# A two-layer mixer and mixture-of-experts block on one core: another order for the opening of the experts, another grouping of routed tiles, and conditioning products in halves

## The chip, the cores and the metric

The kernel runs on one NeuronCore of a Trainium2 chip. The metric is the time of one execution on the device in microseconds; the kernel before took a median of 3143.61 us in three runs (3134.78 to 3149.41).

## The reference, cut to what matters

All arithmetic is float32. Two layers work on 1024 image tokens and 256 context tokens of width 1024. Layer 0 mixes with a gated linear recurrence in both directions, layer 1 with differential attention. Every layer first makes its six conditioning vectors and ends in a mixture of 32 experts, of which every token takes two from one of four groups:

```python
shx1, scx1, gx1, shx2, scx2, gx2 = jnp.split(silu(cond) @ w_mod[layer] + b_mod[layer], 6)
ox, oc = rglru_mixer(...) if layer == 0 else diff_attn_mixer(...)
x = x + gx1 * ox
hx2 = modulate(rms_norm(x, norm2_g[layer]), shx2, scx2)
s = sigmoid(h @ router_w)                        # 32 scores, two experts of the best group
y = sum over the two experts of weight * ((silu(h @ w_gate[e]) * (h @ w_up[e])) @ w_down[e])
x = x + gx2 * y
```

The matrix `w_mod` has 1024 x 6144 elements a layer. An expert has gate and up matrices of 1024 x 512 and a down matrix of 512 x 1024: 6 MB, so 32 experts are 201 MB a layer. Layer 0 routes 1280 tokens, layer 1 the 1024 image tokens.

## The kernel before, in words

The schedule is written out by hand: each engine runs its instructions in the order of the program, and waits are set by the tiles that are written and read. SP issues the loads of weights, POOL issues indirect transfers and many stores.

**Conditioning.** `mod_steps` (L165 on) works through rounds `(layer, r)` of 2048 columns of `w_mod`. A round has eight steps, one for each block of 128 rows; a step loads two tiles of 128 x 1024 and calls `mod_mm` (L143), whose four products of 32 x 512 go to the four 32-column quarters of the PE array and to the four 32-partition quarters of one PSUM bank. Rounds (0, 1), (0, 2), (1, 0), (1, 1), (1, 2) are fillers of layer 0's recurrence stage: after each piece of a projection one step of them is run on PE.

**Output projection and routing.** `post_mixer` goes through the tiles of 128 tokens (ten in layer 0, eight in layer 1). For a tile it computes the projection in two halves of 512 columns, adds each half to the residual (`resid`, L806 and L807), normalises (`norm`, L814 to L820, with the stores of the residual and of `h2d`), transposes, and computes the router's logits (L837). Routing is done for groups of tiles, given as (first tile, count): (0, 4), (4, 3), (7, 3) in layer 0 and (0, 4), (4, 3), (7, 1) in layer 1. After the logits of a group's last tile `router` (L854 to L895) picks two experts for each token on VectorE; `slots`, one call later, ranks the tokens of each expert with products on PE (L903 to L906), writes `row` (L911), adds the counts to `macc` (L913), and issues for each tile and each of the two picks one scatter from POOL (L917) into the slot table `slotd` in DRAM. Behind the last group the counts become blocks of 64 rows (`nblk`, L1019 to L1021). The first expert's six weight chunks of 1 MB are loaded into `raws` during this stage.

**Experts.** `moe` keeps a ring of 20 chunk buffers (`NM`), of which the first six (`NR`) hold the first expert. Buffers 12 to 15 lie in a pool (`pm`) on the left of SBUF, buffers 6 to 11 and 16 to 19 in a pool (`pr`) on its right, ten of 8 KB. On the right there lay before it, from the same end, the projection's weights (`gup`, 64 KB) and its transposed tiles (`pst`, 16 KB), then the routing's own tiles (`pd`). A buffer can be written when what lay there has been read.

The opening (L1219 on) is this: SP and POOL read five experts' block counts from `nblk` (`know`); VectorE clears the halves for gathered rows (L1222); SP loads chunks 6 to 19; POOL loads table 0 (the first 64 slots of every expert) in two halves of 64 partitions (L1076), VectorE halves it into row numbers (L1080), POOL gathers the first rows of expert 0 and of expert 1 (L1102), loads tables 1 to 4, VectorE halves those; PE transposes expert 0's rows (`x_t`, L1109), VectorE copies them (L1110); and POOL gathers expert 0's second rows, if it has more than one block.

Then the loop over the experts: for each block of 64 rows gate and up on PE (L1117, two 64-column halves of the array at once), SiLU on ScalarE, a product on VectorE, transposes, the down product (L1133), scaling on ScalarE (L1139) and an indirect store from POOL (L1141). The next rows' transposes and the previous block's down product are run between the gate and up products and their own transposes. When an expert is done SP refills its buffers.

Of the kernel before, what the change touches and what calls it, by code (L numbers as in the profile page):

```python
# [19 lines left out]
P = 128  # L20
D = 1024
KD = D // P
# [19 lines left out]
ORDER = [g * 8 + i for i in range(8) for g in range(4)]  # L42
NR = 6
NM = 20
B = P // 2
NB64 = 5

# [13 lines left out]
def model(ctx, tc, A, out):  # L61
    nc = tc.nc
# [13 lines left out]
    xd = dram.tile([T, D], F32, name="xd")  # L76
# [10 lines left out]
    side = const.tile([P, 1], F32, name="side")  # L87
    nc.vector.memset(side[:B], 0.0)
    nc.vector.memset(side[B:], 1.0)
    ones = const.tile([P, P], F32, name="ones")  # L90
# [17 lines left out]
    cs = modp.tile([P, KD, 32], F32, name="cs")  # L108
# [18 lines left out]
    def mod_load(l, r, j, eng):  # L127
        res = []
        for h in range(2):
            wm = modp.tile([P, 1024], F32, name="wm", bufs=5)  # L130
            c0 = r * 2048 + h * 1024
            eng.dma_start(wm, A["w_mod"][l].rearrange("(j p) n -> p j n", p=P)[:, j, c0:c0 + 1024])
            res.append(wm)
        return res
# [4 lines left out]
    def mod_bias(l, r, eng):  # L139
        for v in range(2):  # L140
            eng.dma_start(bmod[v:P:32, :], A["b_mod"][l, r * 2048:(r + 1) * 2048].rearrange("(g n) -> g n", g=4))

    def mod_mm(ps, wm, j):  # L143
        for g in range(4):
            nc.tensor.matmul(ps[32 * g:32 * g + 32, :], cs[:, j, :], wm[g // 2][:, (g % 2) * 512:(g % 2 + 1) * 512],
                             start=(j == 0), stop=(j == KD - 1), tile_position=(0, 32 * g))

    def mod_out(l, r, ps):
        mt = modp.tile([P, 512], F32, name="mt", tag="wm", bufs=5)
# [16 lines left out]
    def mod_steps(rounds, pspool, tag, eng, beng, rest, ctag):  # L166

        todo = []
        for l, r in rounds:
            nxt = mod_load(l, r, 0, eng)  # L170
            for step in todo:
                step()
                yield
            mod_bias(l, r, beng)
            for _ in range(rest):
                yield
            ps = pspool.tile([P, 512], F32, name="mps", tag=tag, bufs=1)
            for j in range(KD):
                cur = nxt
                if j + 1 < KD:  # L180
                    nxt = mod_load(l, r, j + 1, eng)
                mod_mm(ps, cur, j)
                if j + 1 < KD:
                    yield
            todo = [lambda l=l, r=r, ps=ps: mod_out(l, r, ps)]
            if r == 0:
                mt = mod_out(l, r, ps)

                def cols(l=l, mt=mt):
                    ps = pspool.tile([P, 512], F32, name="cps", tag=ctag[0], bufs=ctag[1])  # L190
                    mod_cols(l, mt, ps)

                todo = [cols]
            yield
        for step in todo:
            step()
# [63 lines left out]
    raws = {}  # L260
# [425 lines left out]
    def post_mixer(l, N, variant, prep, w_src, x_src, x_dst, groups, w_col=None, head=None, early=None):  # L686
# [332 lines left out]
        nc.tensor.matmul(ct[:, :E], ones, macc, start=True, stop=True)  # L1019
        nc.vector.tensor_scalar(nblk, ct[:, :E], float(B - 1), None, op0=OP.add)  # L1020
        nc.vector.tensor_scalar(nblk, nblk, 6, None, op0=OP.arith_shift_right)  # L1021
# [15 lines left out]
    def x_in(t):  # L1037
        return A["x"][0, t * P:(t + 1) * P, :] if t < XT else A["ctx"][0, (t - XT) * P:(t - XT + 1) * P, :]

    mraw = post_mixer(0, T, lambda t: 0 if t < XT else 1, st0, A["rg_w_out"][0], x_in,  # L1040
                      lambda t: xd[t * P:(t + 1) * P, :], [(0, 4), (4, 3), (7, 3)],
                      early={"w": early, "st": sty, "finish": finish, "release": release})

    def moe(l, N, mraw, raws, keep=False):
# [5 lines left out]
        ps = pool("psM", space=PSUM)  # L1050
        ends = [(6 * E + c) % NM for c in range(4)]
        raws = raws + [(pm if i in ends else pr).tile([P, 2 * D], F32, name=f"wr{i}") for i in range(NR, NM)]
        tabs = pm.tile([P, NB64, E, 3], I32, name="tabs")
        flat = pm.tile([P, 1, 3], I32, name="tabj")
        halves = [w[:, i * 512:(i + 1) * 512] for w in wide for i in range(2)]
# [3 lines left out]
        hm = pm.tile([P, F], F32, name="hm")  # L1059
        ht = pm.tile([P, KF, B], F32, name="ht")  # L1060
        yms = [pm.tile([P, F], F32, name=f"ym{i}") for i in range(2)]
        curs = [pm.tile([P, 3], I32, name=f"cur{i}") for i in range(3)]
        p_x = ps.tile([P, 4, P], F32, name="p_x")
        p_g = ps.tile([P, F], F32, name="p_g")
        p_h = ps.tile([P, KF, B], F32, name="p_h")
        p_y = ps.tile([P, F], F32, name="p_y")
# [3 lines left out]
        h2v = h2d[l][0:N, :].rearrange("n (h d) -> (n h) d", h=2)  # L1070
        ydv = yd[l][0:2 * N, :].rearrange("n (h d) -> (n h) d", h=2)

        def tab_load(j0, j1):

            for h in range(2):
                nc.gpsimd.dma_start(tabs[h * B:(h + 1) * B, j0:j1],  # L1076
                                    slotd[l][j0 * B * E:j1 * B * E, :].rearrange("(j p e) c -> p j e c", p=B, e=E))

        def halve(t):
            nc.vector.tensor_scalar(t[:, :, 0:2], t[:, :, 0:2], 2.0, side, op0=OP.mult, op1=OP.add)  # L1080

        def load(k):

            raw = raws[k % NM]
            e, c = k // 6, k % 6
            if e < E:
                if k < NM:
                    w_chunk(l, raw, ORDER[e], FIRST[c])
                else:
                    with tc.If(used[e] > 0):  # L1090
                        w_chunk(l, raw, ORDER[e], FIRST[c])
            elif keep and k - 6 * E < N // (2 * P):
                c = k - 6 * E
                t = raw.rearrange("p (a d) -> p a d", a=2)
                nc.sync.dma_start(t, xd[2 * c * P:2 * (c + 1) * P, :].rearrange("(a p) d -> p a d", p=P))
                last[2 * c], last[2 * c + 1] = t[:, 0, :], t[:, 1, :]

        def chunk(e, c, j):
            return raws[(6 * e + FIRST.index(c)) % NM].rearrange("p (j f) -> p j f", j=j)

# [5 lines left out]
        def x_t(xb):  # L1106
            xv = xb.rearrange("t (p j) -> t j p", j=4)
            for j in range(4):
                nc.tensor.transpose(p_x[:, j, :], xv[:, j, :], ident)  # L1109
            nc.vector.tensor_copy(xt, p_x)  # L1110
# [50 lines left out]
        def rows_of(e, b):  # L1161
            return xfs[e % 2] if b == 0 else x1s[e % 2] if b == 1 else xms[b % 2]

        def fetch(e, b):

            if e < E:
                if b == 0:
                    gather(rows_of(e, b), tab(e, b)[:, 0:1])
                else:
                    with tc.If(rows[e] > b):  # L1170
                        gather(rows_of(e, b), tab(e, b)[:, 0:1])
# [15 lines left out]
        def finish(e, b, prev):  # L1187
# [27 lines left out]
            with more.Else():  # L1215
                turn(nxt, *prev)
                nc.gpsimd.tensor_copy(curs[e % 2], tab(e, b))

        for e in range(5):  # L1219
            know(e)  # L1220
        for xb in halves:
            nc.vector.memset(xb, 0.0)  # L1222
        for k in range(NR, NM):
            load(k)
        tab_load(0, 1)
        halve(tabs[:, 0])
        fetch(0, 0)
        fetch(1, 0)
        tab_load(1, NB64)
        for j in range(1, NB64):  # L1230
            halve(tabs[:, j])
        x_t(rows_of(0, 0))
        fetch(0, 1)
        for e in range(E):
            n = count(ORDER[e])
            know(e + 5)
# [373 lines left out]
    class last_head:  # L1610
        ps = psF
# [125 lines left out]
```

## Time and profile before

| | us |
|---|---|
| median of three runs | 3143.61 |
| lowest, highest | 3134.78, 3149.41 |
| profiled execution | 3148.4 |
| its span, first to last instruction | 3146.8 |
| PE busy | 2767.8 (88%) |
| VectorE busy | 1373.7 (44%) |
| ScalarE busy | 963.1 (31%) |
| POOL busy | 536.7 (17%) |
| gate and up products L1117, 3456 records | 771.7 |
| down products L1133, 1728 records | 411.7 |
| opening, layer 0: last projection's residual to first gate | 573.7 to 631.3 |
| opening, layer 1: first gate | 2395.6 |

The page's second part divides the span into 40 slices of 78.7 us. PE's digits are 5999989999499999999858999999998985999999991. They read as tenths of the slice in which PE worked. The row DMA gives the mean busy share of the core's 16 DMA engines in the same way. In rows in order of time the first number is the start in us from the span's beginning, the second how long it took; "x4" merges four instructions, and the bracket gives how long the engine stood idle before, and what ended that. A float32 product on PE leaves two records, so that "x8" is four products.

### The profile page before, as it was taken

The numbers are of one execution on the slowest core, as the hardware profiler recorded it, in microseconds if no ns is written. First come the engines' busy times: TensorE is split into PE (matmuls) and PEld (weight loads), VectorE is DVE, ScalarE is ACT, GpSimd is POOL, SyncE is SP. The second block draws the span as 40 slices with busy tenths as digits, with TensorE's granted clock in tenths as the row PEclk, the third lists the DMA queues.
The fourth block names the chain that finished last, engine by engine and source line by source line (L and its number), as shares of the span: only waits on it lengthen the run. The fifth ranks groups of instructions, "written<-read, shape, count | busy, mean of one in ns | idle before, by whom it ended". The sixth has DMA issues, their size and how long they took to land. (4 is left out here: it accounts for less than half of the span.)

```text
span 3146.8 us, 40433 instructions
## 1 busy us (share of the span) xinstructions
PE 2767.8 (88%) x14350; PEld 1703.6 (54%) x14350; DVE 1373.7 (44%) x2597; ACT 963.1 (31%) x1811; POOL 536.7 (17%) x762
## 2 busy tenths in 40 slices
PE   5999989499999999858999999998985999999991
PEld 3667668333333333347888888886872333333330
DVE  6566677411111111187666666666772111111115
ACT  4566652100010010145454544545430110001101
POOL 2121101211111111141101111010012111111113
PEclk8999999699999999969999999998997999999996
DMA  5556465478887897261000000003246877988544
GB/s 195 162 185 205 155 223 181 179 301 316 318 326 288 351 409 302 69 243 50 26 7 26 26 26 27 7 6 129 85 160 258 353 282 310 370 343 346 196 154 178
DMA packets 174213, 611.44 MB, mean 194 GB/s; under 512 B 27336, under 2 KB 80448, under 8 KB 126112
## 3 DMA queue, kind: packets, MB, share of 16 engines
q1 hardware_dynamic: 133328, 493.65, 41.0%
q0 software_dynamic: 40192, 111.96, 9.8%
q8 instruction: 218, 3.57, 0.5%
q14 instruction: 267, 2.19, 0.2%
q10 hardware_dynamic: 208, 0.07, 0.0%
HBM read 560.23 MB, written 64.22 MB: 198 GB/s over the span
## 5 line engine op out<-in xcount | busy, mean ns | idle before, releaser
L1117 PE MATMUL p_g<-wr,xt 128*64 128x512 f32 x3456 | 771.7, 598 | 47.6 <-ACT ym L1139 33.8
L1117 PEld LDWEIGHTS p_g<-wr,xt 128*64 128x64 f32 x3456 | 267.5, 137 | 469.2 <-issue 409.6
L1120 DVE TENSOR_TENSOR hm<-act,p_g 64x512 f32<-64x512 f32 x108 | 74.6, 691 | 832.8 <-ACT act L1119 832.8
L1133 PE MATMUL p_y<-wr,ht 128*64 128x512 f32 x1728 | 411.7, 612 | 23.5 <-issue 22.3
L1119 ACT ACTIVATE act<-p_g 64x512 f32<-64x512 f32 x108 | 63.5, 588 | 851.3 <-PE p_g L1117 851.3
L1133 PEld LDWEIGHTS p_y<-wr,ht 128*64 128x64 f32 x1728 | 118.7, 139 | 234.2 <-issue 220.2
L55 PE MATMUL qkv<-qwh,hth 128*128 128x384 f32 (+1 forms) x640 | 217.2, 339 | 1.3 <-ACT hth L1433 0.5
L56 PE MATMUL qkv<-qwh,htl 128*128 128x384 f32 (+1 forms) x640 | 211.1, 330 | 2.4 <-DVE htl L1438 1.4
L57 PE MATMUL qkv<-qwl,hth 128*128 128x384 f32 (+1 forms) x640 | 210.5, 329 | 0.6 <-DVE qwl L1288 0.6
L1528 DVE TENSOR_REDUCE st<-sc 128x1 f32<-128x1280 f32 x128 | 190.2, 1486 | 21.6 <-PE sc L1515 19.9
L1126 DVE COPY ht<-p_h 128x256 f32<-128x256 f32 x108 | 45.9, 425 | 344.1 <-PE p_h L1125 344.0
L1531 ACT ACTIVATE wide<-sc,st 128x1280 f32<-128x1280 f32 x128 | 168.8, 1324 | 66.2 <-DVE st L1528 66.2
L1554 PE MATMUL po<-V,wide 128*128 128x128 f32 x1280 | 166.6, 288 | 1.4 <-ACT wide L1548 0.5
L1102 POOL DMA_INDIRECT wide<-h2d,tabs x108 | 112.2, 1039 | 319.9 <-issue 70.8
L1554 PEld LDWEIGHTS po<-V,wide 128*128 128x128 f32 x1280 | 156.3, 201 | 13.1 <-ACT wide L1548 12.5
L1548 ACT COPY wide<-wtp 128x512 f32<-128x512 f32 (+1 forms) x192 | 87.8, 522 | 201.2 <-PE wtp L1547 201.1
L1109 PEld LDWEIGHTS p_x<-ident,wide 128*128 128x128 f32 x432 | 60.7, 210 | 141.0 <-issue 92.7
L1560 POOL DMA_DIRECT2D od<-ot x56 | 30.3, 540 | 623.4 <-ACT ot L1557 623.4
L1139 ACT ACTIVATE ym<-p_y,cur 128x512 f32<-128x512 f32 x64 | 44.0, 687 | 289.1 <-PE p_y L1133 226.3
L1512 PE MATMUL sc<-KT,QS 128*128 128x512 f32 (+1 forms) x384 | 117.1, 393 | 15.3 <-ACT KT L1362 11.8
L1109 PE MATMUL p_x<-ident,wide 128*128 128x128 f32 x432 | 81.1, 311 | 54.0 <-DMA wide<-h2d,tabs 48.2
L55 PEld LDWEIGHTS qkv<-qwh,hth 128*128 128x128 f32 x640 | 123.9, 194 | 3.0 <-issue 1.5
(353 smaller groups left out, 4611.2 us busy)
## 6 DMA issues: line engine op xcount, KB each, us to landing
wr<-in_moe_w_gate_dram SPq DMA_DIRECT2D x124, 1024.0 KB, 11.0
wr<-in_moe_w_up_dram SPq DMA_DIRECT2D x124, 1024.0 KB
wr<-in_moe_w_down_dram SPq DMA_DIRECT2D x124, 1024.0 KB, 17.6
wm<-in_w_mod_dram POOLq DMA_DIRECT2D x80, 512.0 KB, 5.5
cy<-yd SPq DMA_DIRECT2D x26, 512.0 KB, 6.9
qraw<-in_da_w_qkv_dram SPq DMA_DIRECT2D x48, 256.0 KB, 3.3
xd<-xres POOLq DMA_DIRECT2D x18, 512.0 KB, 3.9
h2d<-h POOLq DMA_DIRECT2D x18, 512.0 KB, 4.1
```

What stands on the lines that cost most here:

```text
L55: nc.tensor.matmul(ps, lh, rh, start=start, stop=False)
L56: nc.tensor.matmul(ps, ll, rh, start=False, stop=False)
L57: nc.tensor.matmul(ps, lh, rl, start=False, stop=stop)
L1102: nc.gpsimd.indirect_dma_start(out=dst, out_offset=None, in_=h2v, in_offset=bass.IndirectOffsetOnAxis(ap=idx, axis=0), bounds_check=2 * N ...
L1109: nc.tensor.transpose(p_x[:, j, :], xv[:, j, :], ident)
L1117: nc.tensor.matmul(p_g[i * B:(i + 1) * B, :], xt[:, j, h * B:(h + 1) * B], w[i][:, j, :], start=(h == 0 and j == 0), stop=(h == 1 and j == ...
L1133: nc.tensor.matmul(p_y[h * B:(h + 1) * B, :], ht[:, 2 * c + j, :], w[:, j, h * 512:h * 512 + 512], start=(c == 0 and j == 0), stop=(c == 1 ...
L1512: nc.tensor.matmul(o, qs[:, half, :], KT[b][:, half, c0:c0 + n], start=True, stop=False)
L1528: nc.vector.tensor_reduce(st[:, half:half + 1], sc_[:, half, :], AX.X, OP.max)
L1531: nc.scalar.activation(p, sc_[:, half, :], AF.Exp, bias=st[:, 2 + half:3 + half], scale=0.125, accum_out=st[:, 4 + half:5 + half])
L1548: nc.scalar.copy(wT[:, g * 4:g * 4 + n, :], pt[:, 0:n, :])
L1554: nc.tensor.matmul(po[:, 0:P], wT[:, k, :], V[h % 2][:, k, :], start=(k == 0), stop=(k == TT - 1))
```

## The change

Three things are changed.

- `mod_mm` takes a width. For layer 1 it is 256: a step's four products of 512 columns become eight of 256, first the left halves of all four quarters, then the right halves. Layer 0 keeps 512.
- Layer 0's tiles are routed in groups (0, 4), (4, 4), (8, 2).
- The opening of the experts has another order, in both layers. SP issues chunks 6 to 11 first. Table 0 is loaded by POOL and ScalarE, tables 1 to 4 by SP and ScalarE. Table 0 is halved, POOL gathers expert 0's first rows, tables 1 to 4 are halved, then the counts are read, and POOL gathers expert 0's second rows. ScalarE copies one element of those rows into the buffer of chunk 12. SP loads chunks 12 to 19, the first of which is written after that copy. Then come the transposes of expert 0's first rows and the gather for expert 1.

```diff
+NE = 12
...
-    def mod_mm(ps, wm, j):
-        for g in range(4):
-            nc.tensor.matmul(ps[32 * g:32 * g + 32, :], cs[:, j, :], wm[g // 2][:, (g % 2) * 512:(g % 2 + 1) * 512],
-                             start=(j == 0), stop=(j == KD - 1), tile_position=(0, 32 * g))
+    def mod_mm(ps, wm, j, width):
+        for c in range(0, 512, width):
+            for g in range(4):
+                nc.tensor.matmul(ps[32 * g:32 * g + 32, c:c + width], cs[:, j, :],
+                                 wm[g // 2][:, (g % 2) * 512 + c:(g % 2) * 512 + c + width],
+                                 start=(j == 0 and c == 0), stop=(j == KD - 1 and c + width == 512), tile_position=(0, 32 * g))
...
-                mod_mm(ps, cur, j)
+                mod_mm(ps, cur, j, 256 if l == 1 else 512)
...
-                      lambda t: xd[t * P:(t + 1) * P, :], [(0, 4), (4, 3), (7, 3)],
+                      lambda t: xd[t * P:(t + 1) * P, :], [(0, 4), (4, 4), (8, 2)],
...
-        def tab_load(j0, j1):
+        def tab_load(j0, j1, queues):
-            for h in range(2):
-                nc.gpsimd.dma_start(tabs[h * B:(h + 1) * B, j0:j1],
+            for h, eng in enumerate(queues):
+                eng.dma_start(tabs[h * B:(h + 1) * B, j0:j1],
                                     slotd[l][j0 * B * E:j1 * B * E, :].rearrange("(j p e) c -> p j e c", p=B, e=E))
...
+        for k in range(NR, NE):
+            load(k)
+        for xb in halves:
+            nc.vector.memset(xb, 0.0)
+        tab_load(0, 1, (nc.gpsimd, nc.scalar))
+        tab_load(1, NB64, (nc.sync, nc.scalar))
+        halve(tabs[:, 0])
+        fetch(0, 0)
+        for j in range(1, NB64):
+            halve(tabs[:, j])
         for e in range(5):
             know(e)
-        for xb in halves:
-            nc.vector.memset(xb, 0.0)
-        for k in range(NR, NM):
+        fetch(0, 1)
+        nc.scalar.copy(raws[NE][0:1, 0:1], rows_of(0, 1)[0:1, 0:1])
+        for k in range(NE, NM):
             load(k)
-        tab_load(0, 1)
-        halve(tabs[:, 0])
-        fetch(0, 0)
+        x_t(rows_of(0, 0))
         fetch(1, 0)
-        tab_load(1, NB64)
-        for j in range(1, NB64):
-            halve(tabs[:, j])
-        x_t(rows_of(0, 0))
-        fetch(0, 1)
```

## Rows read from the trace of the kernel before

**Rows 1.** busy time by stretch; columns: us, each engine's busy us (instructions), PEclk, DMA share, GB/s.

```profile
605.00:610.00 5.00, 0.00 (x0) 0.00 (x0) 0.00 (x0) 0.00 (x0) 0.38 (x1) 0.50 1.01 422
...
2370.00:2396.00 26.00, 1.54 (x6) 1.03 (x8) 4.00 (x11) 1.05 (x1) 6.30 (x8) 0.50 0.96 365
```

**Rows 2.** instructions in order of time, opening of layer 0's experts; start us, us, engine, line.

```profile
596.87 1.01 POOL L917 DMA_INDIRECT slotd<-row  x1 [13.74 <-DVE macc L913]
...
599.56 0.33 SPq L681 DMA_DIRECT2D wr<-in_moe_w_gate_dram  x1
...
603.31 0.96 POOL L917 DMA_INDIRECT slotd<-row  x1 [0.22 <-issue]
...
609.62 1.14 POOL L1076 DMA_DIRECT2D tabs<-slotd  x2 [5.34 <-DMA slotd<-row]
...
616.34 0.25 DVE L1080 TENSOR_SCALAR tabs<-tabs,side 128x64 int32<-128x64 int32 x1 [14.70 <-DMA tabs<-slotd]
617.39 1.11 POOL L1102 DMA_INDIRECT wide<-h2d,tabs  x1 [6.63 <-DVE tabs L1080]
...
624.50 1.13 PE L1109 MATMUL p_x<-ident,wide 128*128 128x128 f32 x4 [26.62 <-DMA wide<-h2d,tabs]
629.94 0.74 DVE L1080 TENSOR_SCALAR tabs<-tabs,side 128x64 int32<-128x64 int32 x4 [13.35 <-DMA tabs<-slotd]
...
631.33 1.12 PE L1117 MATMUL p_g<-wr,xt 128*64 128x512 f32 x2 [5.70 <-DVE xt L1110]
```

**Rows 3.** order of time, layer 1: routing of one tile, last scatter, first expert.

```profile
2361.27 0.19 DVE L859 TENSOR_TENSOR sm<-sc,rbt 128x32 f32<-128x32 f32 x1
...
2367.93 0.16 DVE L911 SCALAR_TENSOR_TENSOR row<-rank,ei 128x2 int32<-128x2 f32 x1
...
2369.64 0.98 POOL L917 DMA_INDIRECT slotd<-row  x1 [0.22 <-DVE nblk L1021]
...
2388.71 1.14 PE L1109 MATMUL p_x<-ident,wide 128*128 128x128 f32 x4 [19.77 <-DMA wide<-h2d,tabs]
...
2395.59 9.02 PE L1117 MATMUL p_g<-wr,xt 128*64 128x512 f32 x32 [5.74 <-DVE xt L1110]
```

**Rows 4.** PE's waits in layer 0's expert loop: us in total, times, longest.

```profile
PE p_y L1133 <- issue: 14.2, 4, 4.1
```

**Rows 5.** order of time, end of layer 0's output projection and its last routing.

```profile
554.55 0.25 DVE L859 TENSOR_TENSOR sm<-sc,rbt 128x96 f32<-128x96 f32 x1
...
557.70 1.04 PE L830 MATMUL pt<-ident,h 128*128 128x128 f32 x8
...
562.23 0.69 DVE L806 TENSOR_TENSOR o<-o,gate 128x512 f32<-128x512 f32 x1
...
569.42 0.69 DVE L806 TENSOR_TENSOR o<-o,gate 128x512 f32<-128x512 f32 x1
...
573.74 0.69 DVE L806 TENSOR_TENSOR o<-o,gate 128x512 f32<-128x512 f32 x1
...
587.21 0.26 DVE L859 TENSOR_TENSOR sm<-sc,rbt 128x96 f32<-128x96 f32 x1 [6.15 <-ACT sc L854]
...
596.42 0.17 DVE L911 SCALAR_TENSOR_TENSOR row<-rank,ei 128x6 int32<-128x6 f32 x1
```

**Rows 6.** DMA issues of the whole span; KB each, then median us from issue to landing.

```profile
od<-ot POOLq DMA_DIRECT2D x56, 64.0 KB, 1.9
...
slotd<-row POOLq DMA_INDIRECT x36, 2.1
```

**Rows 7.** line L1102 from 2900 to 2930 us, two row gathers: issue to landing.

```profile
DMA to landing us min/median/max: 2.8/5.3/7.8
```

**Rows 8.** order of time, layer 0: the fourth gate and up run.

```profile
667.44 7.09 PE L1117 MATMUL p_g<-wr,xt 128*64 128x512 f32 x32 [0.56 <-ACT ym L1139]
```

**Rows 9.** order of time, PE: one conditioning step of layer 1 and what follows.

```profile
252.25 1.07 PE L145 MATMUL mps<-wm,cs 128*32 128x512 f32 x8
253.25 0.50 PE L55 MATMUL ps_u<-hth,wh 128*128 128x512 f32 x1
```
## The prediction, before the result was known

> **What bounds the kernel now.** I read the profile from coarse to fine. The page's slices first: PE is nearly full but at both ends and in two slices inside the span, both where a layer's experts begin. Next the busy time by stretch: in the 26 us before layer 1's experts PE works 1.54 us while the DMA engines are 0.96 busy, and in layer 0's opening they stand at 1.01 with 422 GB/s [rows 1]. So in these two places the kernel waits for transfers. The order of time then shows for which: in layer 0 PE's first instruction of the experts waits 26.62 us for the gathered rows, and 5.70 us more for VectorE [rows 2]; layer 1 has 19.77 and 5.74 [rows 3]. Behind the opening PE is the bound: its largest wait in layer 0's loop after those two and the short hand-overs from ScalarE is 14.2 us in four pieces that no instruction or transfer ends [rows 4], and none is for weights. A microsecond won in the opening therefore stays won if weights still come in time.
>
> The opening of layer 0 in its order [rows 2]: six last scatters of slots begin at 596.87, the sixth at 603.31. Chunk loads begin at 599.56, behind the counts, and fill the DMA engines. The first table loads are issued at 609.62, land at about 616.3, the gather goes at 617.39 and lands at 624.5. The transposes run at once, but the copy of their result stands on VectorE behind the halving of tables 1 to 4, which waits for its own loads until 629.94. Gate and up begin at 631.33.
>
> **The change, part by part.**
>
> *Groups (4, 4) and (8, 2) in layer 0.* Before, the router of the three-tile group holds VectorE from 554.55 to 562.23 and delays tile 8's second residual, whose product PE has finished by 557.70 [rows 5]. That router goes, so tile 8's residual and norm, which ended when tile 9's first residual began at 569.42 [rows 5], end 4.3 us earlier, near 565.2. Then comes that residual (two instructions of 0.69, 1.4), and now the four-tile router. A tile costs a router and its slots (9.21 - 6.66) / 2 = 1.28 us: three tiles take 587.21 to 596.42 [rows 5], one takes 2361.27 to 2367.93 [rows 3]. Four tiles are thus 7.7 + 1.3 = 9.0, ending at 575.6, where tile 9's second residual stood at 573.74: 1.9 us late, and its norm, transposes and logits with it. The last router has two tiles, 1.3 less. The first last scatter comes at 596.87 + 1.9 - 1.3 = 597.5; the second group's eight scatters follow tile 9's stores on POOL, at 1.29 each, and end near 595, so they are out of the way. Four scatters instead of six: the last starts at 597.5 + 3 x 1.29 = 601.3, 2.0 us earlier than before.
>
> *Six chunks early.* Their buffers lie where the projection's weights and tiles lay (six of 8 KB in the 64 + 16 KB of those pools), all read for the last time before 573.74 (the last product's residual). They need no count, so SP issues them some 25 us earlier; 6.3 MB at 422 GB/s are 15 us, over near 590, behind a routing that uses no transfer in its chain. In layer 1 the same lies ahead of its router. Cost nothing; without this cover (buffers free only at the end of the routing) it is the second case below.
>
> *Quiet tables and gathers.* From the last scatter's start to the first gate, with empty engines:
> 1. the scatter lands: 2.1, median of 36 [rows 6];
> 2. the queue reacts: 0.7 (POOL took 0.8 from the end of the halving to the gather [rows 2]);
> 3. tables land, now from POOL, ScalarE and SP side by side: at least 1.9, like the small stores of attention [rows 6]; at most the 6.7 of before (609.62 to 616.34 [rows 2]); I take 2.4, near the quiet end, since nothing else is in flight;
> 4. halving and gather issue: 1.05 [rows 2];
> 5. the gather lands: 2.8 is the least seen, in a quiet moment [rows 7], 7.1 that of before [rows 2]; I take 3.2;
> 6. transposes, copy, first gate: 1.1 + 0.3 + 0.7 = 2.1, the halving of tables 1 to 4 being over, as their loads went beside the first.
>
> Together 11.6 us. Layer 0: 601.3 + 11.6 = 612.9 against 631.33, so 18.4 less. Layer 1, whose groups are unchanged: 2369.64 + 11.6 = 2381.2 against 2395.59, 14.4 less [rows 3].
>
> *What is late next.* The wait added is on ScalarE: a copy of one element reads the second gather's rows and writes chunk 12's buffer, so SP's last eight loads stand behind that gather. Behind the copy on ScalarE is only the first SiLU, 9 us after the gate begins. On POOL the gather of second rows now follows five register reads (about 2 us): issued near 611, landed near 614, needed at 612.9 + 9. SP then loads 8.4 MB at 422 GB/s, 20 us, until about 635. The third expert, whose run is the fourth (expert 0 has two blocks), began 36.1 us behind the first [rows 2, 8]; its first four chunks are wanted at 649.0. That leaves over 15 us. Expert 0's buffers come free 18 us earlier too, and their reloads queue some 5 us behind, with 30 us to spare.
>
> *Conditioning of layer 1 in halves.* 24 steps (3 rounds of 8), each with eight products of 256 columns instead of four of 512. A step takes PE from 252.25 to 253.25, 1.0 us [rows 9], in which four quarter tiles stream together. Two records of 512 columns in two rounds are 2 x 0.44 (32 records on two half tiles run in 7.09 us [rows 8], so 16 rounds of 0.44); 0.12 is left for entry and drain. The streamed columns stay the same, so the least change is -0.12 a step and the most twice that more, if each extra round pays all of it: -3 to +6 us. I take +0.05 a step, 1.2 us, all of it on the path, since PE is full there. The Trainium skill, "TensorEngine Tiling (Array Packing)", Instruction Overhead, speaks against short pieces: about 60 cycles for each matmul. An estimate from that page is 8 more records x 25 ns x 24 = 4.8 us; the sum would then be 3.6 us worse. No row here has pieces of this width on quarter tiles.
>
> **Sum.** 18.4 + 14.4 - 1.2 = 31.6 us. The profiled execution took 3148.4 us (span 3146.8 and 1.6 around it); it would take 3116.8. It lies 4.8 above the median of the runs, 3143.6, so on that scale I predict 3112.
>
> **The rivals.**
> *The traffic stays.* If the early six buffers wait until the routing is over, tables and gather still meet loads and only VectorE's wait goes: per layer 4.7 us (gate 2.1 behind the transposes of 624.50 and 2388.71, against 631.33 and 2395.59: 4.7 and 4.8), plus 2.0 for the earlier scatters, less 1.2: 10.3, so 3133. For it: these buffers were never used early. Against: the sizes of the pools, and that loads went from 599.56 on while scatters still read the routing's tiles [rows 2].
> *Weights late.* If the eight held loads start only at 646, the third expert waits 7 us in both layers: 3126. It decides from 639 on (649 less 10 us for four chunks); I see the hold end at 615.
> *Slower: quarter tiles no longer overlap at 256 columns.* Then a step is 4 x 0.88 = 3.5 us, 2.5 more, 24 times 60 us: 3112 + 59 = 3171. It decides once a step costs 2.3 us where it costs 1.0 now (24 x 1.3 = 31). Against: the tiles are independent and issued back to back.
> *PE's unexplained stalls.* The 14.2 us of layer 0 in four pieces [rows 4] lie amid straight products. If their place follows the place of the code, the products added ahead of it can move them: with twice as many, and layer 1 like layer 0 at most, up to 28 us, 3140 at worst, or as much won. The Trainium skill, "Runtime: NRT & Kernel Launch", Instruction fetch mechanics, says that a taken branch to code outside the fetched pages stalls the engine; no row shows it here.
>
> **How the numbers follow.** Forecast 0.76; traffic stays 0.09; weights late 0.05; tiles apart 0.07; stalls 0.03. The likeliest alone spans 3100 to 3124. With both landings at their upper ends (4.3 + 3.9 in each layer) and the halves at +6 it is 3133, with all at their lower ends 3106, and stalls moving by two of 3.6 us each reach 3099. I set 3098 to 3131. What a measurement can tell from no change is 0.5%, 15.7 us, thus 3128: faster 0.76 + 0.05 = 0.81; same, 0.09 + 0.03 = 0.12; slower 0.07.
>
> **What would show it.** Right: six loads of SP issued near 574 and near 2343; eight more only after a ScalarE copy, near 615 and 2384; tables landing within 3 us; the four halvings ahead of the transposes; first gate some 11.6 us after the last scatter's start; conditioning steps at 1.05 us. Wrong: a first gate over 16 us after the last scatter, a PE wait before the third expert, steps above 1.3 us.

## The result, and the profile after

The changed kernel's median is 3124.55 us (3113.12 to 3128.07) beside 3148.18 for the kernel before on the same chip: a ratio of 0.9926, interval 0.991 to 0.9941. Measured once more it had 3120.29 beside 3148.86, 0.9912 (0.9894 to 0.993). The forecast was 3112 beside 3143.6, a ratio of 0.9899. So the change is faster, by some 24 to 29 us (0.7 to 0.9%) where 31.6 was expected, and 3124.55 lies inside the range.

The profiled execution took 3128.07 us (span 3126.5), 20.3 less than before. Where they came from, in us, each stretch from the same instruction in both traces:

```
stretch                                     before    after    change   forecast
start to routing's first rank product       529.3     530.1     +0.8    +1.2 (halves)
rank product to layer 0's first gate        102.0      83.5    -18.5   -18.4
layer 0's experts                           694.2     686.4     -7.8     0
to layer 1's last scatter                  1044.1    1046.6     +2.5     0
last scatter to layer 1's first gate         26.0      11.4    -14.5   -14.4
layer 1's experts                           689.0     706.0    +17.0     0
tail                                         62.2      62.4     +0.2     0
```

Both openings came out as worked; what the forecast lacks lies in layer 1's expert loop, which it had left at its length. Layer 0's loop, left at its length too, came out 7.8 us shorter.

The two openings by stretch (us, each engine's busy us, PEclk, DMA share, GB/s), the answer to [rows 1]:

```profile
603.00:612.00 9.00, 0.26 (x1) 0.26 (x2) 1.00 (x5) 0.00 (x0) 2.70 (x3) 0.50 0.23 58
2348.00:2357.00 9.00, 0.81 (x4) 0.73 (x4) 2.49 (x9) 0.00 (x0) 3.13 (x4) 0.50 0.21 58
```

The DMA engines are 0.23 busy where they were full. Layer 0's opening in order of time, the answer to [rows 2] (start us, us, engine, line; in brackets the idle time before and what ended it):

```profile
572.26 0.33 SPq L684 DMA_DIRECT2D wr<-in_moe_w_gate_dram  x1
...
597.95 0.97 POOL L920 DMA_INDIRECT slotd<-row  x1 [3.49 <-DVE macc L916]
...
601.76 0.97 POOL L920 DMA_INDIRECT slotd<-row  x1 [0.23 <-issue]
603.96 1.26 ACTq L1079 DMA_DIRECT2D tabs<-slotd  x2
604.02 0.70 SPq L1079 DMA_DIRECT2D tabs<-slotd  x1
604.48 0.59 POOL L1079 DMA_DIRECT2D tabs<-slotd  x1 [1.75 <-DMA slotd<-row]
607.03 1.06 DVE L1083 TENSOR_SCALAR tabs<-tabs,side 128x64 int32<-128x64 int32 x5 [4.60 <-DMA tabs<-slotd]
608.18 1.10 POOL L1105 DMA_INDIRECT wide<-h2d,tabs  x1 [3.12 <-DVE tabs L1083]
...
611.75 1.13 PE L1112 MATMUL p_x<-ident,wide 128*128 128x128 f32 x4 [13.00 <-DMA wide<-h2d,tabs]
...
613.66 1.12 PE L1120 MATMUL p_g<-wr,xt 128*64 128x512 f32 x2 [0.78 <-DVE xt L1113]
```

From the last scatter's start to the first gate 11.9 us, 28.0 before. The tables go 2.2 after the scatter and land in 3.0, the gather lands 3.6 after its issue, all five halvings are over before the transposes, and the gate waits 0.78 for the copy. Layer 1 has the same picture in 11.4, the answer to [rows 3], with the element copy behind the second gather and the held loads behind that:

```profile
2346.68 0.97 POOL L920 DMA_INDIRECT slotd<-row  x1 [0.21 <-issue]
...
2356.19 1.13 PE L1112 MATMUL p_x<-ident,wide 128*128 128x128 f32 x4 [10.21 <-DMA wide<-h2d,tabs]
...
2358.03 0.19 ACT L1235 COPY wr<-wide 1x1 f32<-1x1 f32 x1 [23.15 <-DMA wide<-h2d,tabs]
2358.10 4.54 PE L1120 MATMUL p_g<-wr,xt 128*64 128x512 f32 x10 [0.78 <-DVE xt L1113]
...
2358.25 0.34 SPq L684 DMA_DIRECT2D wr<-in_moe_w_gate_dram  x1
```

A conditioning step of layer 1 in the order of time, pieces of 256 columns, the answer to [rows 9]:

```profile
410.13 1.07 PE L147 MATMUL mps<-wm,cs 128*32 128x256 f32 x16
411.13 0.50 PE L56 MATMUL ps_y<-hth,wh 128*128 128x512 f32 x1
```

1.00 us to the next product, as before: sixteen records stream in the time of eight. PE's waits in the two loops (us in total, times, longest), first layer 0's, the answer to [rows 4], then layer 1's, and last layer 1's in the kernel before:

```profile
PE p_y L1136 <- issue: 7.4, 3, 2.6
PE p_x L1112 <- issue: 3.6, 6, 1.0
...
PE p_y L1136 <- issue: 10.7, 4, 2.8
PE p_x L1112 <- issue: 7.6, 6, 5.1
...
PE p_y L1133 <- issue: 8.1, 3, 3.2
```

No line there waits for the landing of weights. The pieces that no instruction or transfer ends are still there, but at other places, and with one of 5.1 us in layer 1. The experiments are about these.

### The profile page after: what moved, and what is told of

It is laid out like the page before. It is cut to its first block, busy times and chain, and to the rows that moved or that the text cites. A ratio compares the mean times of both kernels' runs of the same rounds, so it can differ in the third digit from the quotient of the medians.

```text
span 3126.5 us, 40919 instructions
## 1 busy us (share of the span) xinstructions
PE 2770.1 (89%) x14542; PEld 1709.2 (55%) x14542; DVE 1374.5 (44%) x2597; ACT 964.4 (31%) x1813; POOL 532.8 (17%) x756
## 5 line engine op out<-in xcount | busy, mean ns | idle before, releaser
L1144 POOL DMA_INDIRECT yd<-ym,tabs x44 | 44.0, 1000 | 491.0 <-POOLq L1193 309.4
L56 PE MATMUL o<-wh,sth 128*128 128x512 f32 x288 | 118.9, 413 | 7.4 <-DVE xres L810 5.1
```

Source lines behind the costliest of these rows:

```text
L56: nc.tensor.matmul(ps, lh, rh, start=start, stop=False)
```

## The experiments

In all of them theory A is that these waits follow the place of PE's code. Counted from 0 in the traces, the runs of gate and up in a layer (54) give each wait an address that does not depend on the time: 26y is the wait among the down products behind the gates of run 26, x is one at the transposes of the rows, h one at those ahead of the down product, g one at the gates. PE's compiled program is 24576 bytes longer in the changed kernel than with 512 columns; the trace shows instruction packets of 16384 bytes on their own queue, so "place" below is the shift against 512 columns alone, less whole packets. Waits over 1.5 us, without those that a transfer or VectorE ends, from one profiled execution of each kernel:

```
kernel        place   layer 0                        layer 1                               loops, us
before          192*  7y 26y 30y 48y                 5y 19h 25y 52y                        694.2 689.0
w512              0   7y 26y 30y                     26g 52y                               685.0 689.7
pad64             0   7y 26y 30y                     5y 26g 52y                            681.6 687.5
w512_nohold       0   7y 26y 30y 34x                 5y 26g 52y                            686.4 692.5
w512_g33        -64   7y 24x 29y 39y                 20g 26g 39g 52y                       690.3 690.3
w512_pad32     4096   1x 5x 10y 34y 44y              21y 30y 44y 46g                       699.2 687.9
changed        8192   2y 35y 42y                     1x 12y 14g 22y 31y 45y                686.4 706.0
changed_again  8192   2y 20y 35y 42y                 1x 12y 22y 26g 31y 45y                687.1 702.4
w512_pad64     8192   2y 20y 35y 42y                 1x 12y 22y 26g 31y 45y                685.3 698.4
nohold         8192   14h 20y 35y 42y                12y 22y 26g 31y 45y                   685.2 693.7
late6          8192   2y 14h 20y 35y 42y             1x 12y 14g 22y 26g 31y 45y            690.3 697.7
only256        8384*  14y 20y 22y 36y 39x 42y        1g 13y 23y                            704.9 694.7
w512_pad96    12288   18g 22y 24y 28y 39x 40g        23y 36g                               688.9 686.7
* with the opening and the groups of before, whose program is 192 bytes longer than with the new ones
```

The traces bear out the places. Ahead of the loops, where PE's code runs straight, about one packet begins for every 128 of PE's records. Ahead of layer 0's first gate one begins 426 records before it in w512 and in pad64, and in w512_pad32, the changed kernel and w512_pad96 it begins 26, 61 and 91 records earlier than that, where the bytes, at 128 a record, give 32, 64 and 96.

They also show what ends the waits. The loops of the thirteen kernels hold 94 waits over 1.5 us that no instruction or transfer ends. In each of the 94 one packet of the instruction queue comes to its end, and PE goes on 1.17 to 1.73 us later. Such a packet takes about 1 us; the longer waits are those in which it begins late, up to 3.03 us after PE has stopped. Most packets cost nothing of the kind: layer 1's loop in the changed kernel sees 75 of them. The g waits are put down to PE's own sequencer, and a packet ends in each of these too, 2.07 to 2.26 us before PE goes on; not so 1g of only256, which is one of the 94, and 26g of layer 1. The last ends on a branch of SyncE's around a chunk's load (SPq L1093), stands there at both places, takes 1.2 us in the changed kernel too, and is no wait of this kind.

**w512: 512 columns again.**

```diff
-                mod_mm(ps, cur, j, 256 if l == 1 else 512)
+                mod_mm(ps, cur, j, 512)
```

> The changed kernel with layer 1's conditioning back in pieces of 512 columns; nothing else differs. Theory A (the forecast's missing 10 us are stalls of PE whose place follows the place of its code): the two openings keep 11.9 and 11.4 us from the last scatter to the first gate, a conditioning step is 1.00 us either way, and yet the experts' loops (686.4 and 706.0 us in the changed kernel) come out different by 4 to 15 us each, since 96 products fewer lie ahead of them; the whole anywhere between 3112 and 3140. Rival B (the pieces themselves cost time that the step does not show): both loops as in the changed kernel within 3 us, and the whole 8 to 12 us shorter, near 3114.

3107.95 us, ratio 0.9893 (0.9873 to 0.9912); loops 685.0 and 689.7, both openings as in the changed kernel (11.85 and 11.53). The steps stand at 1.00:

```profile
410.23 1.06 PE L147 MATMUL mps<-wm,cs 128*32 128x512 f32 x8
411.22 0.50 PE L56 MATMUL ps_y<-hth,wh 128*128 128x512 f32 x1
```

So the gain of leaving the pieces out is not in the step but in a loop 1900 us later. The ratio is the lowest of the study, though not told apart from that of w512_g33, and its interval touches those of the changed kernel. The time alone fits B better (some 6 to 10 us by the ratios); A's own bounds are missed, with layer 0's loop only 1.4 us from the changed kernel's, layer 1's 16.3, and the whole below 3112. The places speak for A, since all waits but 26g are at places of the kernel before, and B's equal loops are not there. Separating them needs the next runs.

**pad64: 64 more small transposes at the start of the changed kernel.**

```diff
+    for _ in range(64):
+        nc.tensor.transpose(vps[:, :16], crow, ident[:16, :16])
     nc.tensor.transpose(vps[:, :16], crow, ident[:16, :16])
```

> The changed kernel with 64 more of the first small transpose (16 by 16) at the start, where PE has no work for 11.5 us; they write the same values again. Theory A (place of the code): nothing moves before the first loop, the openings stay, but the stalls of PE in the two loops come at other points and the loops differ from 686.4 and 706.0 by 4 us or more, either way; largest single stall still 2 to 5 us. Rival C (the stalls come from what the loops do: the held loads, the order of experts): they come at the same experts, within 3 us the same loops, and the time is that of the changed kernel, 3125.

3112.93, ratio 0.9908 (0.9886 to 0.9931). The pieces of 256 are all there, and yet layer 1's loop is 687.5 and not 706.0. The 64 transposes add 8192 bytes, 24576 + 8192 are two packets exactly, and every long wait stands at a run where w512 or the kernel before has one: by the loops B and C fall, and A gets its sharp form. The whole time can't decide it: this ratio is not told apart from the changed kernel's 0.9912 in its second measurement, and the profiled execution, 3108.49, is among the fast ones of six (3106.81 to 3120.8). The transposes are not free, as I had expected: the 64 take 6.97 us, and the first product behind them comes at 19.44 and not 14.81, some 2 us late at the output projection.

**w512_pad64, w512_pad32, w512_pad96: the same pad with 512 columns.** The edit is the one above, with 64, 32 and 96, on w512.

> Layer 1's conditioning back at 512 columns, and 64 of the small transposes added at the start: PE's code then ends 8192 bytes later than with 512 columns alone, which is where the changed kernel has it, within one 16384-byte packet of the instruction queue (there 24576 bytes later, by 96 more products). Theory A, sharpened (a stall comes where a branch of PE's loop meets the seam of such a packet, so only the place modulo 16384 bytes counts): the stalls of the changed kernel come back, at 36, 187, 451 and 545 us behind layer 0's first gate and at 25 (5 us, beside the held loads), 168, 301, 421 and 599 us behind layer 1's; loops near 686 and 706; the whole near 3122, 12 to 15 us longer than with 512 columns alone. Rival B (the pieces of 256 columns cost the time by themselves): as with 512 columns alone, stalls at 98, 337 and 393 us behind layer 0's first gate, loops near 685 and 690, the whole near 3108.

3126.19, ratio 0.9937 (0.9916 to 0.9957): with the columns of before, the slow layer 1 of the changed kernel (698.4, beside 706.0 and 702.4 in its two profiles), and the list of its second profile run by run. This interval and w512's (0.9873 to 0.9912) do not meet. Its profile is 18 us longer than w512's (by the ratios it is some 14): about 2 are the pad itself and 9 the loops; the rest lies in the routing of layer 0 (3) and between the layers (4), and was not followed up.

> 512 columns and 32 of the small transposes at the start, 4096 bytes more of PE's code, a place that no kernel has had. Theory A, sharpened: stalls at other points than in either family (98, 337, 393 or 36, 187, 451, 545 us behind layer 0's first gate), a loop that is 0 to 10 us off 685 and 690; openings as before, 11.9 and 11.5 us. Rival B: the points and loops of 512 columns alone, 3108 within 3 us.

3128.33, 0.9939 (0.9917 to 0.9961). New places, as A says; layer 0's loop is 14 longer than w512's, more than the 10 that I allowed, with waits of 4.7 and 5.3 us at 1x and 5x.

> 512 columns and 96 of the small transposes, 12288 bytes more of PE's code. Theory A, sharpened: a fourth set of points, loops 0 to 10 us off 685 and 690, 3100 to 3125. Rival B: 3108 within 3 us, with the points of 512 columns alone.

3116.05, 0.9902 (0.9884 to 0.9919). A fourth list, and the loops within 4 us of w512's; the pad's own cost (10.4 us of transposes at the start, 5.5 of it still there at the output projection) makes most of the rest.

**only256: the kernel before with the pieces alone.** The edit is the diff's first part.

> The kernel before with nothing changed but layer 1's conditioning in pieces of 256 columns: PE's code gets 24576 bytes longer, one and a half packets of 16384. Theory A: a step costs 1.00 us as before, the openings stay at 28 and 26 us, and the stalls of PE's loops leave the points of the kernel before (100, 339, 396 and 623 us behind layer 0's first gate) for those of the changed one (187, 451 and 545; in layer 1 168, 301, 421 and 599). No stall of 5 us at 25 in layer 1, since no held loads are under way there. The whole 3135 to 3152. Rival B (the pieces cost time by themselves): 8 to 12 us longer than before, 3151 to 3156, with the points of the kernel before.

3164.4 beside 3148.86, ratio 1.0048 (1.0032 to 1.0065). Slower by more than either theory said. Chains of 28.2 and 25.3 us as before; loops longer by 10.7 and 5.7. The waits have left the list of before, which B cannot give; but only some of them are at those of the changed kernel (20y, 42y), so a list is fixed for one program, not for a place of the packet alone to 192 bytes. In w512_g33, 64 bytes from w512, only 7y of layer 0's three is kept, and 24x, 29y and 39y are new. How a list comes about inside a packet is open. PE's waits of layer 0's loop, against the 14.2 in 4 of before:

```profile
PE p_y L1135 <- issue: 17.0, 6, 4.8
```

**nohold and w512_nohold: without ScalarE's copy.**

```diff
-        nc.scalar.copy(raws[NE][0:1, 0:1], rows_of(0, 1)[0:1, 0:1])
```

> The changed kernel without ScalarE's one-element copy, so that SP's eight chunk loads follow the tables at once, near 606 us, and run beside the gathers. Theory D (the hold is what keeps the gathers quiet): the first gather takes 5 to 8 us instead of about 3, the first gate comes 2 to 5 us later in each layer, the whole 4 to 10 us longer, 3129 to 3135. Rival C (the held burst of eight loads is what stalls PE, as in the 5.1 us in front of layer 1's first transposes for the second run of an expert): the gates stay within 1 us, that stall goes and layer 1's loop is 5 us or more shorter, near 3118. Theory A has the stalls of the loops move by nothing, since no PE instruction is added or removed.

3121.16, 0.9926 (0.9904 to 0.9947). Both theories hold in part. The first gates come 15.8 and 15.5 us behind the scatters; the order of time in layer 0, where the loads had begun 1.6 us before the gather:

```profile
605.33 1.09 POOL L1105 DMA_INDIRECT wide<-h2d,tabs  x1 [3.19 <-DVE tabs L1083]
...
612.75 1.13 PE L1112 MATMUL p_x<-ident,wide 128*128 128x128 f32 x4 [16.90 <-DMA wide<-h2d,tabs]
```

The gather lands 7.4 us after its issue, beside 3.6 in quiet. So the hold is worth 3.9 and 4.1 us in the chains, as D says; but the whole is not longer, as C says: the ratio is that of the changed kernel, and layer 1's loop is 693.7 where that had 706.0 and 702.4. And of the five lists at place 8192 this one alone lacks the 1x of layer 1. The same transposes in the changed kernel, in its second run, in w512_pad64 and, last, in nohold:

```profile
2382.97 1.10 PE L1112 MATMUL p_x<-ident,wide 128*128 128x128 f32 x4 [5.11 <-issue]
```

```profile
2378.84 1.10 PE L1112 MATMUL p_x<-ident,wide 128*128 128x128 f32 x4 [5.08 <-issue]
```

```profile
2388.43 1.10 PE L1114 MATMUL p_x<-ident,wide 128*128 128x128 f32 x4 [5.21 <-issue]
```

```profile
2380.82 0.72 PE L1112 MATMUL p_x<-ident,wide 128*128 128x128 f32 x4 [0.31 <-issue]
```

Place and burst make this one together: w512 has the burst and not the place, and at its run there is no wait at all:

```profile
2373.12 0.75 PE L1112 MATMUL p_x<-ident,wide 128*128 128x128 f32 x4
```

In the changed kernel PE stops at 2377.86. Its traffic from 2376 to 2382 (forty slices, then the instruction packet):

```profile
DMA  9797999999799999997969596939592612023111
...
q8 instruction: 1, 0.02, 1.1%
```

That packet begins at 2380.42, when the held loads have just drained, and PE goes on at 2382.97; in nohold it begins at 2378.08, ahead of the need. That the fetch queued behind the burst is my reading of these times; the trace does not show when it was asked for. Nor does such a length need the held loads: w512_g33 has 5.5 us at 24x and w512_pad32 5.3 us at 5x, both in layer 0 and among the loop's own loads. The DMA engines are busy at a share of 0.96 or more around 93 of the 94 waits.

> 512 columns and no copy on ScalarE, so the eight later loads follow the tables at once. Theory D (the hold keeps the gathers quiet; its burst hurts only where a packet of PE's instructions is fetched in it, which with 512 columns it is not): first gates 15.8 and 15.5 us behind the last scatters, not 11.9 and 11.5, loops near 685 and 690 as with the hold, the whole 6 to 9 us longer than with it, 3114 to 3117. Rival C (the burst itself delays the loops): what the gates lose comes back in the loops, 3108 within 3 us.

3118.6, 0.9904 (0.9884 to 0.9925); gates 16.2 and 15.5 behind the scatters, the loops 4 longer together. As D says, with a little more: at a place without 1x the hold gains some 8 us in the chains. By the ratios the whole is 3.5 us longer than w512, within the noise.

**late6: the six early loads wait for the counts again.**

```diff
+        for e in range(5):
+            used[e] = count(ORDER[e], (mybir.EngineType.SP,))
         for k in range(NR, NE):
             load(k)
...
         for e in range(5):
-            know(e)
+            rows[e] = count(ORDER[e], (mybir.EngineType.Pool,))
```

> The changed kernel with SP's five reads of the counts put back ahead of its six early chunk loads, so that these wait for the end of the routing as before and meet the tables and the first gather; the hold stays. Theory of the forecast (empty DMA engines are worth 5 to 7 us in each layer, VectorE's order the other 5): from the last scatter to the first gate 16 to 23 us instead of 11.9 and 11.4, the whole 10 to 20 us longer, 3135 to 3145. Rival (only VectorE's order counts; table and gather land as fast beside loads): the gates within 2 us of the changed kernel's, the whole within 4 us of 3125.

3145.41, ratio 1.0005 (0.9991 to 1.0019): the whole gain is gone. Layer 0's opening in order of time, then ten us of it by stretch:

```profile
600.53 1.19 SPq L687 DMA_DIRECT2D wr<-in_moe_w_down_dram  x2
605.32 1.24 ACTq L1079 DMA_DIRECT2D tabs<-slotd  x2
...
612.16 0.26 DVE L1083 TENSOR_SCALAR tabs<-tabs,side 128x64 int32<-128x64 int32 x1 [11.78 <-DMA tabs<-slotd]
613.22 1.10 POOL L1105 DMA_INDIRECT wide<-h2d,tabs  x1 [6.79 <-DVE tabs L1083]
618.22 0.74 DVE L1083 TENSOR_SCALAR tabs<-tabs,side 128x64 int32<-128x64 int32 x4 [5.80 <-DMA tabs<-slotd]
...
620.53 1.98 PE L1120 MATMUL p_g<-wr,xt 128*64 128x512 f32 x4 [0.78 <-DVE xt L1113]
```

```profile
604.00:614.00 10.00, 0.00 (x0) 0.00 (x0) 0.26 (x1) 0.00 (x0) 1.37 (x2) 0.50 1.02 404
```

Scatter to gate takes 20.8 and 22.1 us. Tables issued at 605.3 land 6.8 later (3.0 in quiet) and the gather in 5.4 (3.6); the scatter itself releases POOL 3.4 us later than in quiet. So of the 16.1 us by which layer 0's chain is shorter in the changed kernel 8.9 come from empty DMA engines and 7.2 from the rest (VectorE's order, the tables on three queues, the hold); in layer 1 10.7 and 3.9. Those 7.2 and 3.9 are in this run too, but its loops (5 more than before) and the way between the layers (7 more) take them back. That way, from layer 0's last product to layer 1's last scatter, takes 1044.1 to 1051.2 us over the thirteen kernels, and what sets it is open.

**w512_g33: layer 0's groups back.**

```diff
-                      lambda t: xd[t * P:(t + 1) * P, :], [(0, 4), (4, 4), (8, 2)],
+                      lambda t: xd[t * P:(t + 1) * P, :], [(0, 4), (4, 3), (7, 3)],
```

> 512 columns, and layer 0's groups back to (0, 4), (4, 3), (7, 3): PE's code is 64 bytes shorter than with 512 columns alone, so nearly the same place. Forecast's term: the last scatter and with it the first gate of layer 0 come 2.0 us later (six scatters behind the last router instead of four, a router of three tiles instead of two), the chain behind it stays 11.9, the loops stay within 3 us: 3110. Rival (the larger second group delays tile 9 by as much as the smaller last one wins): the last scatter within 0.5 us of the place with (4, 4), (8, 2).

3112.71, 0.9896 (0.9879 to 0.9913). Counted from the span's start the last scatter comes 1.1 earlier, which looks like neither; but the whole first layer of this execution runs 3.4 us early, by the first rank product, ahead of which nothing differs. Order of time, first here, then in w512:

```profile
524.41 0.39 PE L906 MATMUL rk<-mt,upper 128*128 128x128 f32 x2
...
598.37 0.96 POOL L920 DMA_INDIRECT slotd<-row  x1 [0.23 <-issue]
```

```profile
527.80 0.39 PE L906 MATMUL rk<-mt,upper 128*128 128x128 f32 x2
...
599.43 0.97 POOL L920 DMA_INDIRECT slotd<-row  x1 [0.22 <-issue]
```

73.96 against 71.63: the new groups win 2.3 us, the same as in the changed kernel against before (74.0 and 71.7). The ratios do not show so little. Layer 0's loop is 5.3 us longer than w512's, not within the 3 expected.

**changed_again: the changed kernel a second time.** 3120.29, ratio 0.9912. The waits are at the runs of its first profile, but for 14g (0.8 us now) and 20y (3.3 us, none before), and layer 1's loop is 702.4: what places them is not chance.

## Why the prediction came out so

**What bounds it: right.** Both openings waited for transfers and for VectorE's order, and what was won there stayed won: the rest of the trace is earlier by it, except where PE's own waits and its granted clock changed. The slices were misread in one point. The page's row for the kernel before has 40 digits:

```profile
PE   5999989499999999858999999998985999999991
```

It has three low slices inside the span, 4, 5 and 5, and only the first and the last are where experts begin; in the middle one (from 1338 us) PE waits for VectorE at the start of layer 1's mixer.

**Groups: right.** 2.0 earlier forecast, 2.3 measured from the rank product on. Tile 9's residual stands at 575.85, forecast 575.6.

**Early loads and quiet engines: right, 18.4 and 14.4 forecast, 18.5 and 14.5 measured** (the first from the rank product on). Of the six steps of the chain the landings were under-sized by 0.6 (tables, 3.0 for 2.4) and 0.4 (gather, 3.6 for 3.2), and the halving and issue overlapped a little more. late6 shows the rival in which the traffic stays: I had given it -10.3 us in all, 9.5 of them in the chains; its chains win 11.1, and the time nothing.

**The hold: right in its place, incomplete in its cost.** The held loads go at 614.78 and 2358.25, no expert waits for weights. What is late next was not weights but PE's code: one wait of 5.1 us in layer 1 that ends on an instruction packet.

**The step that failed is the term for the conditioning halves,** "I take +0.05 a step, 1.2 us". As a price of the step it was too high: 1.00 us either way, +0.1 in all. The Trainium skill, "TensorEngine Tiling (Array Packing)", Instruction Overhead, has about 60 cycles for each matmul, 4.8 us by the forecast's estimate; this trace does not show them. As a price of the edit it was far too low: with the openings of before, 15.5 us by medians (only256, +0.48%), with the new ones 0.2 to 0.3% by ratio, 6 to 10 us (w512 against the changed kernel's two measurements, whose intervals touch w512's). The lists of waits, and w512_pad64, which makes the loss with no pieces at all, put it down to 24576 more bytes of PE's code ahead of the loops. The forecast had this as its last rival, at 0.03 and with the right sign of doubt: "If their place follows the place of the code". It deserved far more, since [rows 4] already showed waits that nothing ended. That the time still fell within the range is in part luck: by the place alone the kernel comes at a ratio of 0.9893 (w512) or 0.9937 (w512_pad64, 2 us of it the pad's). The Trainium skill, "Runtime: NRT & Kernel Launch", Instruction fetch mechanics, says that a taken branch to code outside the fetched pages stalls the engine; the trace agrees in part. The 94 waits end on instruction packets, and most come behind the branch that follows a run's gates; but only 9 are at the first instruction there, and 80 stand among the down products, behind four transposes and at least two more records, which no run here explains.

**Sum.** Openings -33.0 (forecast -32.8), loops +9.2 (0), before the routing +0.8 and the way between the layers +2.5 (together +1.2): -20.3 in the profiles, -31.6 forecast. The +2.5 is not the change's: the changed kernel's second profile has 1044.6 us there, beside 1044.1 before.

**A wait costs more than its length.** By stretch, the changed kernel around a wait of 2.56 us that ends at 1064.77:

```profile
1062.00:1066.00 4.00, 1.45 (x7) 0.48 (x8) 0.00 (x0) 0.00 (x0) 1.12 (x2) 0.97 1.01 404
1066.00:1070.00 4.00, 3.79 (x10) 1.01 (x6) 0.17 (x1) 0.59 (x1) 0.00 (x0) 0.60 1.02 418
1070.00:1074.00 4.00, 3.65 (x18) 1.61 (x20) 0.25 (x1) 0.10 (x1) 1.19 (x2) 1.00 1.02 420
```

Behind the wait PE's granted clock is 0.60 for 4 us, that is mostly at the lower of its two levels (1.2 and 2.4 GHz), and ten of PE's records are done where eighteen are done in the next four: by estimate some 1.6 us (4 x 0.4) lost besides. Of the 94 waits 64 have such a fall within 8 us behind them, worth 1.4 to 3.4 us each, and 30 have none; in the 4 us ahead of them the clock is full. Over the thirteen kernels a layer's loop grows by 1.3 to 1.6 us for each us of waits above 0.8 that no transfer ends (a straight line through them, correlation 0.92 in each layer).

The traces close the account of the loops. Take from a loop's length all of PE's waits above 0.8 us and the time that the granted clock cost (its lacking share times the time): what is left is 664.7 to 670.1 us in layer 0 and 666.4 to 671.9 in layer 1, in all thirteen kernels. In layer 1 the change raised the waits from 12.8 to 21.1 us and the clock's cost from 7.1 to 14.3, together 15.6 of the 17.0. In layer 0 they fell from 15.2 to 11.6 and from 12.0 to 7.6, together the whole of the 7.8. The clock's part is not fixed by the code: in its second profile the changed kernel pays 9.1 in layer 1.

## What to carry to other kernels

Where small dependent loads decide a start, keep bulk loads out of their way on both sides: those that depend on nothing go ahead of the chain, the rest behind the last small one; here that and an order of VectorE's instructions gave 30.6 us (16.1 and 14.5). An edit that adds instructions to an engine whose loops branch is priced by its own time and also by the shift that it gives the code behind it, so compare a change with the same change shifted by less than a packet before it is called good or bad. Where a trace shows waits that nothing ends, find their ordinal in the loop rather than their time, which shows whether two kernels stall at the same instruction, and see whether an instruction packet ends in each of them.

## What the hardware showed that was not expected

- The same products stall PE at the same run of a loop in nearly all profiled executions with one place of the code (layer 0's 35y and 42y in all five, 2y in four; the 1x of layer 1, in the four with held loads: 5.11, 5.08, 5.21 and, in late6, 5.15 us), and a shift of its code by 8192 bytes moves nearly all of them; a shift by 32768 bytes leaves nearly all where they are. All 94 waits of the thirteen traces end 1.17 to 1.73 us behind an instruction packet of 16384 bytes.
- Pieces of 256 columns on four quarter tiles stream as fast as pieces of 512, to 0.5%: 1.001 and 0.996 us a step.
- A row gather lands 3.6 us after its issue with no loads under way and 7.4 us beside loads that began 1.6 us earlier.
- The recurrent layer ends some 3 us earlier or later from one execution to the next (419.4 to 423.3 us) with nothing different ahead of it, so a term of 2 us is read from a near instruction and not from the span's start.
